# Ten instead of six pairs of layer 1's up projections by seven half-size products, summed in PSUM chains, and the scaled copies of h moved behind the last square

## The chip, the cores and the metric

The kernel runs on one core of a Trainium2 chip. Its engines are TensorE (PE for matmuls, PEld for the loads of their stationary side), VectorE (DVE), ScalarE (ACT), GpSimd (POOL) and SyncE (SP, which here only issues DMAs). The metric is device time of one execution in microseconds (us). All data are float32; most matmuls run on float32 values split into a high and a low part, three products for one.

## The reference

A trunk of two decoder layers on 512 tokens of width 1024. Layer 0 is a conformer convolution and a SwiGLU feed-forward part; layer 1 is sliding-window attention and another feed-forward part. The change lies in the second feed-forward part alone:

```python
def rmsnorm(x, g):
    return x * rsqrt(mean(x * x, -1) + EPS) * g

def swiglu_ffn(x, w_up, w_down):              # w_up: 1024 x 5632, w_down: 2816 x 1024
    gate, up = split(x @ w_up, 2, axis=-1)
    return (silu(gate) * up) @ w_down

h = h + attn @ w_o                            # the end of attention
h = h + swiglu_ffn(rmsnorm(h, norm_ffn[1]), ffn_w_up[1], ffn_w_down[1])
out = rmsnorm(h, norm_final)
```

## The kernel before

The hidden width 2816 is cut into eleven pairs of two 128-wide blocks. `STEPS1` (line 37) writes the order of layer 1 out by hand: up 0, up 1, up 2, low 0, up 3, up 4, low 2, and so on to up 9, up 10, low 8. "up p" makes the gated hidden values of pair p, "low p" multiplies two pairs, p and p + 1, with their part of `w_down` and adds to h. The last pair, 10, goes through a plain down projection at the end (line 1451).

A plain pair (`plain_pair`, line 741) takes four weight chunks of 128 x 1024 values. Each chunk is 8 weight blocks, each block three matmuls (`mm3`, line 352: high times high, high times low, low times high) over 512 tokens. A pair by sevens (`seven_pair`, line 772) multiplies in Strassen-Winograd's way: a 2 x 2 split of weights and of tokens, seven products of 256 tokens each instead of eight. It takes seven chunks: three blocks of the weights (A11, A12, A22) and four sums of blocks (S1 to S4). Against them stand B11, B21 of h and four differences of h (T1 to T4). Before the change, pairs 1, 3, 5, 6, 8 and 9 go this way (`SEVENS`, line 57), each product has a PSUM bank of its own, and ACT, DVE and POOL put the four output quarters c11, c12, c21, c22 together (lines 786 to 800). The low units (`low_pairs`, line 833) already use chains: `CHAINS` (line 827) names three banks, x, y and z. In x the products A11, S2, S3 and A22 are added one after the other, in z S1 and S4, and what stands in the bank after each is read out before the next is added.

The weights come through `advance` (line 278), called once per chunk. It moves the making of sums one step on (`prepare`, line 252: each sum takes two steps; a copy of one block inside DRAM on SP's queue, placed behind the latest load, then a transfer from POOL's queue that adds the other block in DRAM), issues loads up to six chunks ahead into four raw buffers (line 247, SP), and splits up to three chunks ahead: ACT casts raw to the high part (line 273), DVE subtracts to get the low part (line 276). Sums begin in layer 0's second feed-forward part, four for each unit by sevens, up or low.

The seam is the end of attention and pair 0. While `w_o`'s last products come out, DVE adds them to h (line 1410), and for each of h's eight row blocks `Rows.on_h` (line 719) splits the row scaled by the norm's gain (ACT line 510, DVE line 511), squares it on ACT (line 463) and adds the squares on DVE (line 467). `Rows.sums` (line 723), a generator that `plain_pair` drives in pair 0, makes eight scaled copies of h on ACT (line 726), the four differences T on POOL (line 732), and their splits on ACT and DVE (lines 515 to 519). The norm's factor goes through PE (line 477), POOL (line 481), DVE (line 484) and PE (line 503). During pair 1, eight `flip`s (line 1421) transpose h on PE.

Behind the products of a pair, DVE (line 806), ACT (807) and POOL (808) gate the hidden values, POOL makes the forms that low units need (`forms_of`, line 813, POOL line 822), and ACT and DVE split them (lines 515 to 519).

The order of instructions on each engine is made by a scheduler of the framework from the program's order and its own estimate of times. `issue_after(x)` adds an order, no wait: what is traced inside comes behind x on x's engine.

Of the kernel before, what the change touches and what calls it, by code (L numbers as in the profile page):

```python
# [14 lines left out]
ALU = mybir.AluOpType  # L15
# [8 lines left out]
FT = FF // P  # L24
# [28 lines left out]

SEVEN = ("A11 B11", "S3 T3", "S1 T1", "S2 T2", "A12 B21", "S4 B22", "A22 T4")
SEVENS = (1, 3, 5, 6, 8, 9)
SEVEN_FIRST = ("A11 B11", "S1 T1", "S3 T3", "S2 T2", "A12 B21", "S4 B22", "A22 T4")
SEVEN_LOW = ("A11 B11", "S1 T1", "S2 T2", "A12 B21", "S3 T3", "S4 B22", "A22 T4")


def by_seven(layer, pair):
    return layer == 1 and pair in SEVENS


def order_of(kind, pair):
    if kind == "low":
        return SEVEN_LOW
    return SEVEN_FIRST if pair == SEVENS[0] else SEVEN


def ups(layer, pair):
# [4 lines left out]


def blocks_of(kind, pair):
    return [(kind, pair, n.split()[0]) for n in order_of(kind, pair)]  # L80


def is_block(c):
# [116 lines left out]
def hybrid_trunk(ctx: ExitStack, tc: tile.TileContext, xT, W, prm_in, wdw_in, sinks, relb, onehot, fin, lead, out):  # L200
    nc = tc.nc
# [10 lines left out]
    def uid(s):  # L212
        ctr[0] += 1
        return f"{s}{ctr[0]}"

    def bank():
        return ps.tile([P, 512], F32, tag="bank", name=uid("bank"))

    def quad(dt=F32R):
        return quads.tile([P, 4, 512], dt, tag="quad", name=uid("quad"))  # L220

    def temp():
        return tmp.tile([P, 512], F32, tag="tmp", name=uid("tmp"))
# [69 lines left out]
    def get_seven(kind, pair, n):  # L293

        advance()
        u = stream["use"]
        stream["use"] += 1
        assert PLAN[u] == blocks_of(kind, pair)[n]
        return splits.pop(u)
# [49 lines left out]
        sh = dict(a=n)  # L349
        return tuple(w and w.rearrange("p (a b) -> p a b", **sh) for w in (hi, lo))  # L350

    def mm3(out, w, x, start, stop):
        if w[1] is None:
            nc.tensor.matmul(out, w[0], x, start=start, stop=stop)  # L354
            return
        nc.tensor.matmul(out, w[0], x[0], start=start, stop=False)  # L356
        nc.tensor.matmul(out, w[0], x[1], start=False, stop=False)  # L357
        nc.tensor.matmul(out, w[1], x[0], start=False, stop=stop)  # L358

    class Act:  # L360
        def __init__(self, n, w=512):
# [33 lines left out]
    h = [hT[:, i, :] for i in range(KT)]  # L395
# [53 lines left out]
    def col(name, i):  # L449
        c = PARAM_COLS[name] + i  # L450
        return prm[:, c:c + 1]


    class Rms:
# [5 lines left out]

        def add(self, t):
            sq = temp()[:, 0:self.w]
            nc.scalar.square(sq, t)  # L463
            if self.acc is None:
                self.acc = sq
            else:
                self.eng.tensor_add(sq, self.acc, sq)  # L467
                self.acc = sq
# [44 lines left out]
    def split(dst, src, negative=False):  # L513
        if negative:
            nc.scalar.mul(dst[0], src, -1.0)
            nc.vector.scalar_tensor_tensor(dst[1], src, -1.0, f32(dst[0]), op0=ALU.mult, op1=ALU.subtract)
            return
        nc.scalar.copy(dst[0], src)
        nc.vector.tensor_sub(dst[1], src, f32(dst[0]))
# [190 lines left out]
    class Rows:  # L710
# [12 lines left out]
        def sums(self):  # L723
            f = [quad(F32) for _ in range(2)]
            for i in range(KT):
                nc.scalar.mul(f[i // 4][:, i % 4, :], h[i], col(self.gain, i))
            b11, b12, b21, b22 = (x[:, :, s] for x in f for s in HALF)
            t1 = self.pool.tile([P, 1024], F32, tag="sum", name=uid("t1"), bufs=1).rearrange("p (k s) -> p k s", k=4)

            for name, t, f, a, b in (("T1", t1, nc.gpsimd.tensor_sub, b11, b12), ("T3", b12, nc.gpsimd.tensor_sub, b22, b12),  # L730
                                     ("T2", b11, nc.gpsimd.tensor_add, b12, b11), ("T4", b21, nc.gpsimd.tensor_sub, b11, b21)):
                f(t, a, b)
                yield
                both = quads.tile([P, 2, 4, 256], F32R, tag="quad", name=uid("rows"))
                self.block[name] = [both[:, a] for a in range(2)]
                split(self.block[name], t, name == "T2")

    def new_gates(pool):
        return pool.tile([P, 2, 2, 2, 256], F32, tag="up", name=uid("up"), bufs=3)
# [32 lines left out]
    def seven_pair(pair, rows, pool, between=None):  # L772

        c = new_gates(pool)
        c11, c12, c21, c22 = (c[:, m, s] for m in range(2) for s in range(2))
        acc = {}
        for n, name in enumerate(order_of("up", pair)):
            w = [x.rearrange("p (a k c) -> p a k c", a=2, k=4) for x in get_seven("up", pair, n)]
            a, b = name.split()
            x = rows.block[b]  # L780
            r = acc[a] = bank().rearrange("p (a s) -> p a s", a=2)
            for which in range(2):
                for k in range(4):
                    mm3(r[:, which], [v[:, which, k, :] for v in w], [x[e][:, k, :] for e in range(2)],
                        which == 0 and k == 0, which == 1 and k == 3)
            if a == "A11":
                nc.scalar.copy(c11, r)
            elif a == "S1":
                nc.scalar.copy(c22, r)
            elif a == "S2":  # L790
                nc.vector.tensor_add(c12, r, c11)
                nc.vector.scalar_tensor_tensor(c21, acc["S3"], -1.0, c12, op0=ALU.mult, op1=ALU.subtract)
                nc.gpsimd.tensor_add(c12, c12, c22)
                nc.gpsimd.tensor_sub(c22, c21, c22)
            elif a == "A12":
                nc.vector.tensor_add(c11, r, c11)
            elif a == "S4":
                nc.vector.tensor_add(c12, r, c12)
            elif a == "A22":
                nc.vector.tensor_sub(c21, c21, r)  # L800
            if between is not None:
                between()
        rs_bc = rows.rms.step2().rearrange("p (s q) -> p s q", s=2)
        for m in range(2):
            gate = c[:, m, :, 0, :]
            nc.vector.tensor_mul(gate, gate, rs_bc)
            nc.scalar.activation(gate, gate, AF.Silu)
            nc.gpsimd.tensor_mul(gate, gate, c[:, m, :, 1, :])
        return c
# [3 lines left out]
    def forms_of(c, pool, odd):  # L813
# [9 lines left out]
        for part in (slice(0, 2), slice(3, 4), slice(4, 8)):  # L823
# [3 lines left out]
    CHAINS = {"A11": ("x", 0, 0), "S1": ("z", 1, 1), "S2": ("x", 0, 1), "A12": ("y", 0, 0), "S3": ("x", 1, 1),  # L827
              "S4": ("z", 0, 1), "A22": ("x", 1, 0)}

    def rows_of(g, t):  # L830
        return hT[:, g * 4:(g + 1) * 4, t * P:(t + 1) * P]

    def low_pairs(pair, forms, rs):

        chains = {}
        for n, name in enumerate(order_of("low", pair)):
            whi, wlo = get_seven("low", pair, n)
            a, b = name.split()
            chain, g, s = CHAINS[a]
            first = chain not in chains  # L840
            if first:
                chains[chain] = [bank() for _ in range(2)]
            for t, out in enumerate(chains[chain]):
                for e in range(2):
                    xh, xl = (f[:, FORM[b], t * P:(t + 1) * P] for f in forms[e])
                    ws = slice(e * 512, (e + 1) * 512)
                    for i, (x, w) in enumerate(((xh, whi), (xh, wlo), (xl, whi))):
                        nc.tensor.matmul(out, x, w[:, ws], start=first and e == 0 and i == 0, stop=e == 1 and i == 2,  # L848
                                         skip_group_check=True)
                to, scale = rows_of(g, 2 * s + t), (rs[1] if g else rs[0])[:, 2 * s + t:2 * s + t + 1]  # L850
                src = out.rearrange("p (i c) -> p i c", i=4)
                if a == "A12":
                    m = temp()
                    nc.scalar.mul(m, out, scale)
                    nc.gpsimd.tensor_add(to, to, m.rearrange("p (i c) -> p i c", i=4))
                else:
                    nc.vector.scalar_tensor_tensor(to, src, scale, to, op0=ALU.mult, op1=ALU.add)
# [22 lines left out]
    with tc.tile_pool(name="conv", bufs=2) as cv:  # L880
# [234 lines left out]
        first = [Pw1(0, 0, raw, turn=True)]  # L1115
# [104 lines left out]
    if True:  # L1220
        ffn_part(0, 1, x0["ffn0"], ALL, Both(), nxt.on_h)
        x, rms = nxt.x, nxt.rms
# [31 lines left out]
        for n in range(4):  # L1254
            nc.vector.tensor_scalar(vq[:, n].rearrange("p a g c -> p (a g c)"), vb[n][:, 0:256], rs[:, n:n + 1], None,
                                    op0=ALU.mult)
# [126 lines left out]
        for part in range(2):  # L1383
            for g in range(2):
# [23 lines left out]
                for m in range(4):  # L1408
                    i = g * 4 + m
# [19 lines left out]
    for kind, pair in STEPS1:  # L1429
# [6 lines left out]
        if by_seven(1, pair):  # L1436
            c = seven_pair(pair, nxt, pool7, flip if pair == SEVENS[0] else None)
        else:
            c = plain_pair(pair, nxt, pool7)
        if pair == SEVENS[0]:  # L1440
            flip()
# [10 lines left out]
    for b in range(NBLK):  # L1452
# [3 lines left out]
        for g, (whi, wlo) in enumerate(whole):  # L1456
            acc = bank()
# [50 lines left out]
```

## Time and profile before

| | |
|---|---|
| median of 3 runs | 1071.57 us (1064.79 to 1073.39) |
| the profiled execution | 1072.48 us |
| its span, first to last instruction | 1070.1 us |
| granted TensorE clock, mean | 0.994 |
| PE busy | 1054.9 us (99%) |
| DVE, ACT, POOL busy | 748.5, 554.1, 432.8 us |
| HBM read and written | 181.64 and 51.38 MB |

The page of the profile gives busy time by engine, 40 slices of the span with the granted clock (PEclk) and the DMA engines' busy share, the DMA queues, and the chain of work that ended last. Rows of the timeline read: start in us, duration in us, engine, line, operation, output<-inputs, shape, count, and in brackets the engine's idle time before it with what ended it. A matmul's duration is its latency; matmuls overlap, so the distance of two starts is what one costs. In this execution attention ends at about 711 us, pair 0 runs to 742, layer 1's other pairs and low units to 1056.

### The profile page before, as it was taken

Reading aid. Unit: us, or ns where it says so; the run is one execution under the profiler, and the core shown is the slowest. Engines: PE = TensorE matmul, PEld = TensorE weight load, DVE = VectorE, ACT = ScalarE, POOL = GpSimd, SP = SyncE. Lnnn points to the kernel's source line nnn. Section 1 sums busy time; section 2 is a strip of 40 time slices with the busy share of each in tenths; the row PEclk is TensorE's granted clock in tenths of the full one; section 3 lists DMA queues with packets and bytes.
Section 4 is the critical chain, followed back from the end, with each engine's and each line's share of the span. In section 5 each row is a group of like instructions: output and inputs, shape, how many; then the busy total and the mean of one; then the engine's idle time right before and its main releaser. Section 6 shows DMA issues by size and latency. Waiting matters only on the chain.

```text
span 1070.1 us, 16002 instructions
## 1 busy us (share of the span) xinstructions
PE 1054.9 (99%) x5878; PEld 917.0 (86%) x5878; DVE 748.5 (70%) x1159; ACT 554.1 (52%) x968; POOL 432.8 (40%) x523
## 2 busy tenths in 40 slices
PE   9999999999999999999999999998999999999996
PEld 7888889999988888888888877777989899898985
DVE  3999988977777644444436466487767778768867
ACT  3887888755565333222343565474544355444543
POOL 3999998710321312211212344123532415315401
PEclk9999999999999999999999999998999999999998
DMA  9238046565556777676766444455989655545532
GB/s 356 86 98 98 3 141 214 178 230 184 177 183 191 236 203 211 169 211 190 189 188 188 138 109 137 118 158 158 277 229 332 213 188 179 157 156 177 180 118 79
DMA packets 52059, 187.92 MB, mean 176 GB/s; under 512 B 6188, under 2 KB 12493, under 8 KB 51277
## 3 DMA queue, kind: packets, MB, share of 16 engines
q1 hardware_dynamic: 44924, 162.74, 46.4%
q0 software_dynamic: 6336, 23.07, 12.6%
q8 instruction: 46, 0.75, 0.3%
q10 hardware_dynamic: 720, 1.10, 0.3%
q14 instruction: 33, 0.26, 0.1%
HBM read 181.64 MB, written 51.38 MB: 218 GB/s over the span
## 4 chain that ended last, share of the span: by engine, by line
PE 96%; DVE 2%; ACT 1%; issue 1%; DMA 1%; POOL 0%; SPq 0%
PE bank L356 19%; PE bank L357 19%; PE bank L358 19%; PE bank L906 10%; PE bank L848 9%; PE bank L388 5%; PE bank L354 4%; PE bank L389 3%; PE bank L1304 1%; PE bank L1346 1%; PE bank L1333 1%; PE bank L1004 1%; DMA both<-in_lead_dram 1%; PE bank L894 1%; PE bank L1461 0%
## 5 line engine op out<-in xcount | busy, mean ns | idle before, releaser
L276 DVE TENSOR_TENSOR wlo<-raw,whi 128x1024 fp32r<-128x1024 f32 x219 | 299.7, 1371 | 175.2 <-ACT whi L273 174.1
L273 ACT CAST whi<-raw 128x1024 fp32r<-128x1024 f32 x219 | 229.6, 1049 | 311.7 <-PE bank L357 199.7
L357 PE MATMUL bank<-quad,whi 128*128 128x512 f32 (+1 forms) x1008 | 349.8, 347 | 3.9 <-DVE quad L511 3.9
L356 PE MATMUL bank<-quad,whi 128*128 128x512 f32 (+1 forms) x1008 | 350.1, 348 | 0.0
L358 PE MATMUL bank<-quad,wlo 128*128 128x512 f32 (+1 forms) x1008 | 349.4, 347 | 0.0
L357 PEld LDWEIGHTS bank<-quad,whi 128*128 128x128 f32 x1008 | 191.5, 190 | 27.5 <-DVE quad L511 4.3
L356 PEld LDWEIGHTS bank<-quad,whi 128*128 128x128 f32 x1008 | 191.6, 190 | 24.8 <-issue 1.6
L358 PEld LDWEIGHTS bank<-quad,wlo 128*128 128x128 f32 x1008 | 191.5, 190 | 23.9 <-issue 0.6
L948 POOL TENSOR_TENSOR pr<-pr,pr 128x256 f32<-128x256 f32 x208 | 156.9, 812 | 6.6 <-ACT pr L947 6.6
L955 DVE SCALAR_TENSOR_TENSOR bank<-apad,wdw,bank 128x256 f32<-128x256 f32 x248 | 112.4, 484 | 3.4
L947 ACT ACTIVATE pr<-apad,wdw 128x256 f32<-128x256 f32 x208 | 98.2, 501 | 14.8 <-POOL pr L948 13.0
L906 PE MATMUL bank<-quad,w 128*128 128x256 f32 x448 | 98.7, 380 | 0.0
L906 PEld LDWEIGHTS bank<-quad,w 128*128 128x128 f32 x448 | 84.9, 190 | 11.8 <-DVE bank L955 0.2
L388 PE MATMUL bank<-quad,whi 128*128 128x512 f32 x212 | 75.9, 398 | 0.0
L268 POOL DMA_DIRECT2D sum<-in_W_dram x22 | 18.3, 833 | 123.0 <-DMA sum<-in_W_dram 122.8
L822 POOL TENSOR_TENSOR up<-up 128x256 f32<-128x256 f32 x40 | 44.2, 1114 | 43.0 <-DVE up L768 41.4
L268 POOL DMA_DIRECT2D sum<-sum x22 | 18.0, 818 | 105.8 <-DMA sum<-in_W_dram 104.3
L389 PE MATMUL bank<-quad,wlo 128*128 128x256 f32 x212 | 59.3, 280 | 0.0
L467 POOL TENSOR_TENSOR tmp<-tmp,tmp 128x256 f32<-128x256 f32 (+1 forms) x28 | 27.0, 963 | 79.1 <-ACT tmp L463 62.8
L848 PE MATMUL bank<-wlo,fhi 128*128 128x512 f32 x140 | 55.1, 393 | 0.0
L356 PE MATMUL bank<-rows,whi 128*128 128x256 f32 x192 | 54.6, 285 | 0.0
L358 PE MATMUL bank<-rows,wlo 128*128 128x256 f32 x192 | 54.3, 283 | 0.0
(220 smaller groups left out, 1603.3 us busy)
## 6 DMA issues: line engine op xcount, KB each, us to landing
raw<-in_W_dram SPq DMA_DIRECT2D x187, 512.0 KB, 3.8
sum<-in_W_dram SPq DMA_DIRECT2D x44, 512.0 KB, 5.4
raw<-sum SPq DMA_DIRECT2D x44, 512.0 KB, 3.9
sum<-in_W_dram POOLq DMA_DIRECT2D x22, 512.0 KB, 6.6
sum<-sum POOLq DMA_DIRECT2D x22, 512.0 KB, 6.4
w<-in_W_dram SPq DMA_DIRECT2D x14, 512.0 KB, 9.0
fd<-fs SPq DMA_DIRECT2D x1, 3072.0 KB, 34.1
h<-in_xT_dram SPq DMA_DIRECT2D x8, 256.0 KB, 8.4
```

The lines of the kernel that those rows point to most:

```text
L273: on_act = nc.scalar.copy(hi, src).ins
L276: latest[:] = [on_act, lo_engine[0].tensor_sub(lo, src, f32(hi)).ins]
L356: nc.tensor.matmul(out, w[0], x[0], start=start, stop=False)
L357: nc.tensor.matmul(out, w[0], x[1], start=False, stop=False)
L358: nc.tensor.matmul(out, w[1], x[0], start=False, stop=stop)
L388: nc.tensor.matmul(first[2], first[0], first[1], start=start, stop=False)
L389: nc.tensor.matmul(second[2], second[0], second[1], start=False, stop=stop)
L848: nc.tensor.matmul(out, x, w[:, ws], start=first and e == 0 and i == 0, stop=e == 1 and i == 2, skip_group_check=True)
L906: mm = nc.tensor.matmul(self.pb[:, w * W2:(w + 1) * W2], w1_of(ct, w, k), x[k] if x else xg[k][:, tok], start=k == 0, stop=k == KT - 1)
L947: on_act = nc.scalar.mul(pr, a[:, j:j + W2], tap(j))
L948: on_pool = nc.gpsimd.tensor_add(pr, acc, pr)
L955: on_dve = nc.vector.scalar_tensor_tensor(yt if i == nd - 1 else c, src, tap(i), c if i else self.shift, op0=ALU.mult, op1=ALU.add)
```

## The change

Three things are changed.

- All pairs of layer 1 but the first go by sevens: 2, 4, 7 and 10 join the six. Four more units are 16 more sums of weights. One order of the products holds for all, that of the low units: A11, S1, S2, A12, S3, S4, A22. `Rows.sums` makes T2 second, from B22 and T1.
- The seven products of an up pair go to three banks by `CHAINS`. What is read out: A11 is copied to c11 (ACT), S1 to c22 with the sign turned (ACT), S2 to c12 (ACT), A12 added to c11 (DVE), S3 subtracted from c22 (DVE), S4 added to c12 (DVE), A22 copied to c21 with the sign turned (ACT). The two operations on POOL and two on DVE are gone.
- ACT's eight scaled copies of h (`Rows.sums`) are ordered behind the last square of `Rows.on_h`.

```diff
--- before.py
+++ after.py
@@ -53,22 +53,13 @@
 
 
 
-SEVEN = ("A11 B11", "S3 T3", "S1 T1", "S2 T2", "A12 B21", "S4 B22", "A22 T4")
-SEVENS = (1, 3, 5, 6, 8, 9)
-SEVEN_FIRST = ("A11 B11", "S1 T1", "S3 T3", "S2 T2", "A12 B21", "S4 B22", "A22 T4")
-SEVEN_LOW = ("A11 B11", "S1 T1", "S2 T2", "A12 B21", "S3 T3", "S4 B22", "A22 T4")
-
+SEVEN = ("A11 B11", "S1 T1", "S2 T2", "A12 B21", "S3 T3", "S4 B22", "A22 T4")
+SEVENS = tuple(range(1, FT // 2))
 
 def by_seven(layer, pair):
     return layer == 1 and pair in SEVENS
 
 
-def order_of(kind, pair):
-    if kind == "low":
-        return SEVEN_LOW
-    return SEVEN_FIRST if pair == SEVENS[0] else SEVEN
-
-
 def ups(layer, pair):
     return [("up", layer, pair, half, which) for half in range(2) for which in range(2)]
 
@@ -77,7 +68,7 @@
 
 
 def blocks_of(kind, pair):
-    return [(kind, pair, n.split()[0]) for n in order_of(kind, pair)]
+    return [(kind, pair, n.split()[0]) for n in SEVEN]
 
 
 def is_block(c):
@@ -349,13 +340,13 @@
         sh = dict(a=n)
         return tuple(w and w.rearrange("p (a b) -> p a b", **sh) for w in (hi, lo))
 
-    def mm3(out, w, x, start, stop):
+    def mm3(out, w, x, start, stop, **kw):
         if w[1] is None:
             nc.tensor.matmul(out, w[0], x, start=start, stop=stop)
             return
-        nc.tensor.matmul(out, w[0], x[0], start=start, stop=False)
-        nc.tensor.matmul(out, w[0], x[1], start=False, stop=False)
-        nc.tensor.matmul(out, w[1], x[0], start=False, stop=stop)
+        nc.tensor.matmul(out, w[0], x[0], start=start, stop=False, **kw)
+        nc.tensor.matmul(out, w[0], x[1], start=False, stop=False, **kw)
+        nc.tensor.matmul(out, w[1], x[0], start=False, stop=stop, **kw)
 
     class Act:
         def __init__(self, n, w=512):
@@ -460,7 +451,7 @@
 
         def add(self, t):
             sq = temp()[:, 0:self.w]
-            nc.scalar.square(sq, t)
+            self.squared = nc.scalar.square(sq, t).ins
             if self.acc is None:
                 self.acc = sq
             else:
@@ -723,12 +714,13 @@
         def sums(self):
             f = [quad(F32) for _ in range(2)]
             for i in range(KT):
-                nc.scalar.mul(f[i // 4][:, i % 4, :], h[i], col(self.gain, i))
+                with tc.issue_after(self.rms.squared):
+                    nc.scalar.mul(f[i // 4][:, i % 4, :], h[i], col(self.gain, i))
             b11, b12, b21, b22 = (x[:, :, s] for x in f for s in HALF)
             t1 = self.pool.tile([P, 1024], F32, tag="sum", name=uid("t1"), bufs=1).rearrange("p (k s) -> p k s", k=4)
 
-            for name, t, f, a, b in (("T1", t1, nc.gpsimd.tensor_sub, b11, b12), ("T3", b12, nc.gpsimd.tensor_sub, b22, b12),
-                                     ("T2", b11, nc.gpsimd.tensor_add, b12, b11), ("T4", b21, nc.gpsimd.tensor_sub, b11, b21)):
+            for name, t, f, a, b in (("T1", t1, nc.gpsimd.tensor_sub, b11, b12), ("T2", b11, nc.gpsimd.tensor_add, b22, t1),
+                                     ("T3", b12, nc.gpsimd.tensor_sub, b22, b12), ("T4", b21, nc.gpsimd.tensor_sub, b11, b21)):
                 f(t, a, b)
                 yield
                 both = quads.tile([P, 2, 4, 256], F32R, tag="quad", name=uid("rows"))
@@ -773,31 +765,33 @@
 
         c = new_gates(pool)
         c11, c12, c21, c22 = (c[:, m, s] for m in range(2) for s in range(2))
-        acc = {}
-        for n, name in enumerate(order_of("up", pair)):
+        chains = {}
+        for n, name in enumerate(SEVEN):
             w = [x.rearrange("p (a k c) -> p a k c", a=2, k=4) for x in get_seven("up", pair, n)]
             a, b = name.split()
-            x = rows.block[b]
-            r = acc[a] = bank().rearrange("p (a s) -> p a s", a=2)
+            x, chain = rows.block[b], CHAINS[a][0]
+            first = chain not in chains
+            if first:
+                chains[chain] = bank().rearrange("p (a s) -> p a s", a=2)
+            r = chains[chain]
             for which in range(2):
                 for k in range(4):
                     mm3(r[:, which], [v[:, which, k, :] for v in w], [x[e][:, k, :] for e in range(2)],
-                        which == 0 and k == 0, which == 1 and k == 3)
+                        first and which == 0 and k == 0, which == 1 and k == 3, skip_group_check=True)
             if a == "A11":
                 nc.scalar.copy(c11, r)
             elif a == "S1":
-                nc.scalar.copy(c22, r)
+                nc.scalar.mul(c22, r, -1.0)
             elif a == "S2":
-                nc.vector.tensor_add(c12, r, c11)
-                nc.vector.scalar_tensor_tensor(c21, acc["S3"], -1.0, c12, op0=ALU.mult, op1=ALU.subtract)
-                nc.gpsimd.tensor_add(c12, c12, c22)
-                nc.gpsimd.tensor_sub(c22, c21, c22)
+                nc.scalar.copy(c12, r)
             elif a == "A12":
                 nc.vector.tensor_add(c11, r, c11)
+            elif a == "S3":
+                nc.vector.tensor_sub(c22, c22, r)
             elif a == "S4":
                 nc.vector.tensor_add(c12, r, c12)
             elif a == "A22":
-                nc.vector.tensor_sub(c21, c21, r)
+                nc.scalar.mul(c21, r, -1.0)
             if between is not None:
                 between()
         rs_bc = rows.rms.step2().rearrange("p (s q) -> p s q", s=2)
@@ -833,7 +827,7 @@
     def low_pairs(pair, forms, rs):
 
         chains = {}
-        for n, name in enumerate(order_of("low", pair)):
+        for n, name in enumerate(SEVEN):
             whi, wlo = get_seven("low", pair, n)
             a, b = name.split()
             chain, g, s = CHAINS[a]
```

## The prediction

> **What bounds the kernel now.** I read the page first (busy shares, granted clock, DMA share, chain of work), then busy time by stretch for layer 1's feed-forward part, then the timelines of PE, ACT, DVE and POOL where the page shows a dip, then the DMA queues.
>
> ```profile
> span 1070.1 us, 16002 instructions
> PE 1054.9 (99%) x5878; PEld 917.0 (86%) x5878; DVE 748.5 (70%) x1159; ACT 554.1 (52%) x968; POOL 432.8 (40%) x523
> PEclk9999999999999999999999999998999999999998
> DMA  9238046565556777676766444455989655545532
> PE 96%; DVE 2%; ACT 1%; issue 1%; DMA 1%; POOL 0%; SPq 0%
> sum<-in_W_dram SPq DMA_DIRECT2D x44, 512.0 KB, 5.4
> ```
>
> PE is the bound: 99% busy and 96% of the chain. So time falls only if PE gets fewer matmul steps or loses an idle stretch, and it rises if PE has to wait for something new. Two places in the page matter: the one slice in mid-kernel where the clock falls to 8, and three DMA slices (9, 8, 9) right behind it. The last row is the copies that begin the weight sums: 44, four for each of eleven units taken by seven products.
>
> ```profile
> 10.00:30.00 20.00, 20.00 (x97) 17.65 (x96) 10.01 (x24) 8.52 (x21) 8.00 (x12) 1.00 1.04 400
> 711.00:742.00 31.00, 27.12 (x108) 21.71 (x107) 23.22 (x19) 15.81 (x21) 13.71 (x7) 0.89 0.52 141
> 798.00:838.00 40.00, 40.00 (x257) 36.48 (x256) 30.89 (x32) 18.57 (x23) 17.91 (x16) 1.00 1.03 318
> 871.00:908.00 37.00, 37.00 (x310) 36.96 (x309) 32.05 (x33) 19.84 (x25) 16.11 (x11) 1.00 0.58 185
> ```
>
> The columns are the stretch, its length, busy time of PE, PEld, DVE, ACT and POOL, the clock, the DMA share and GB/s. In 711:742 (pair 0, the seam) PE misses 3.9 us and its clock is down. In 871:908 (pairs 5 and 6, seven products each, no sums being made) nothing is missing. In 798:838 PE is full too, but the DMA engines are at 1.03 with 318 GB/s; with plain loads alone (10:30) they moved 400.
>
> **The change, part by part.** The sum is made against the profiled execution: 1070.1 us of span and 2.4 around it, 1072.5 us, which is 0.9 above the median of the three runs (1071.57).
>
> *Products of pairs 2, 4, 7 and 10.* A plain pair is 4 chunks x 8 x 3 = 96 matmuls of 512 columns; a pair by sevens is 7 x 8 x 3 = 168 of 256 columns.
>
> ```profile
> 742.14 0.28 PE L357 MATMUL bank<-quad,whi 128*128 128x256 f32 x1
> ...
> 744.77 0.28 PE L358 MATMUL bank<-quad,wlo 128*128 128x256 f32 x1
> ```
>
> ```profile
> 767.93 0.39 PE L357 MATMUL bank<-quad,whi 128*128 128x512 f32 x1
> ...
> 771.33 0.39 PE L357 MATMUL bank<-quad,whi 128*128 128x512 f32 x1
> ```
>
> The first pair of rows lies 22 steps apart, 2.63 us, so 0.1195 us a step; the second 15 steps, 3.40 us, 0.2267. A plain pair takes 96 x 0.2267 = 21.8 us, one by sevens 168 x 0.1195 = 20.1. Four pairs save 4 x 1.7 = 6.7 us. It is a small gain because seven products of half the width are 7/8 of the work and a step of 256 is a little over half a step of 512.
>
> *The seam.* What stops PE in 711:742 is one DVE instruction:
>
> ```profile
> 720.59 0.61 PE L356 MATMUL bank<-quad,whi 128*128 128x512 f32 x2
> 725.08 0.50 PE L357 MATMUL bank<-quad,whi 128*128 128x512 f32 x1 [3.88 <-DVE quad L511]
> ```
>
> ```profile
> 727.82 0.77 PE L356 MATMUL bank<-quad,whi 128*128 128x512 f32 x1
> ...
> 732.66 0.45 PE L358 MATMUL bank<-quad,wlo 128*128 128x512 f32 x1
> ```
>
> ```profile
> 711.87 0.68 DVE L1410 TENSOR_TENSOR h<-bank,h 128x512 f32<-128x512 f32 x1
> 715.62 3.19 DVE L276 TENSOR_TENSOR wlo<-raw,whi 128x1024 fp32r<-128x1024 f32 x1 [2.47 <-ACT whi L273]
> 719.40 2.88 DVE L467 TENSOR_TENSOR tmp<-tmp,tmp 128x512 f32<-128x512 f32 x1
> 722.21 2.82 DVE L511 SCALAR_TENSOR_TENSOR quad<-h,prm,quad 128x512 fp32r<-128x512 f32 x1
> ```
>
> ```profile
> 715.04 2.68 POOL L732 TENSOR_TENSOR t<-quad 128x1024 f32<-128x1024 f32 x1
> 719.24 2.49 POOL L732 TENSOR_TENSOR quad<-quad,quad 128x1024 f32<-128x1024 f32 x1 [1.52 <-ACT quad L726]
> ```
>
> ```profile
> 710.87 3.78 ACT L726 ACTIVATE quad<-h,prm 128x512 f32<-128x512 f32 x6
> 714.55 1.03 ACT L273 CAST whi<-raw 128x1024 fp32r<-128x1024 f32 x1
> 715.49 0.72 ACT L510 ACTIVATE quad<-h,prm 128x512 fp32r<-128x512 f32 x1
> ```
>
> The last row of h is ready at 712.55, but ACT first makes six scaled copies (3.78 us), so the split of h's last two rows starts at 715.49. The copies also let POOL start its differences at 715.04, and DVE's instructions beside them take 2.8 to 3.2 us. So the last low half ends at 725.03 and PE idles 3.88 us. Then it runs at half speed: 4.84 us for eleven steps that take 2.49 at 0.2267, 2.35 us lost. With the copies behind the last square, ACT after 710.87 does one cast, two splits and two squares (some 3.7 us, to 714.6), DVE follows by about 716.5, and PE wants those rows at 719.2 and 720.6: no wait. I take off 3.88 + 2.35 = 6.2 us. Bounds: nothing saved (POOL's differences hit another instruction PE needs) and 7.0 (the eight tiny matmuls behind the gap also run cold). I take nearly all, since the margin is 4 us.
>
> What now comes later: eight copies at 0.63 us put T1 at about 717.5 instead of 715.0, and four POOL operations of some 2.6 us end near 729. T1's rows are wanted at the second product of pair 1, which starts at 735.4 + 2.9 with the 6.2 us gone, T2's 2.9 later (it moves up by one product), T3's at the fifth. On ACT the casts of pair 0 wait behind the copies, at 5.4 us a chunk; on POOL the power of the norm waits behind at most two differences, 5 us, against 8 us that it was early (it is needed with the pair's last product). Both cost nothing; if that cover goes, some 2 us.
>
> For the clock, the gap of 3.88 us is the only one in mid-kernel and the half-speed steps follow it. The Trainium skill, TensorE: Matmul & The Clock Gate, Part 1, says that an idle window of about 3.4 us drops the clock to half. By that rule shorter waits cost their own length only and the sum stays as it is; if waits elsewhere gather to that length, each would cost about 2.35 us more.
>
> *Evacuations and chains.* The six old pairs lose three DVE/POOL steps and gain two ACT copies (0.58 us each); POOL loses two operations per pair. The four new ones add three casts (1.05) and three subtractions each, while PE's time per pair stays 20 us and DVE is at 32 of 37 in 871:908 where all pairs are of this kind. Nothing here is a bound: 0 us. One wait is new: product 3 writes the bank of product 1, 5 that of 3, 7 that of 5, so each evacuation must be done within one product, 2.9 us.
>
> ```profile
> 868.07 1.05 ACT L273 CAST whi<-raw 128x1024 fp32r<-128x1024 f32 x1 [1.70 <-PE bank L357]
> 869.02 0.58 ACT L787 COPY up<-bank 128x512 f32<-128x512 f32 x1
> ```
>
> A cast stands in front of the copy on ACT: 1.05 + 0.58 of 2.9 us, so 1.2 us to spare. It holds, as long as the cast's own data are there.
>
> *The sums of weights.* Four more units are 16 more copies on SP's queue, 16 more accumulating transfers on POOL's, and 12 more loads on SP's. One sum starts every second chunk, so their pace is set by PE.
>
> ```profile
> q1 hardware_dynamic: 1959, 9.55, 60.2%
> q0 software_dynamic: 864, 3.15, 42.6%
> ```
>
> ```profile
> sum<-in_W_dram SPq DMA_DIRECT2D x35, 512.0 KB, 5.2
> ```
>
> ```profile
> 825.60 1.05 ACT L273 CAST whi<-raw 128x1024 fp32r<-128x1024 f32 x1 [3.38 <-DMA raw<-in_W_dram]
> ```
>
> ```profile
> 787.59 16.48 PE bank L848 x72
> ```
>
> The first two rows are the queues in 798:838, the third the copies issued up to 766, where pair 2 begins. At 0.524 MB a transfer, q1 moved 18.2 and q0 6.0 in 40 us: exactly the mix of a sum and its two loads (three to one), so the full DMA engines need 6.6 us per sum. PE asks for one per two chunks: 5.74 us in a pair, and 5.5 in a low unit (12 matmuls of 0.229 a chunk, by the last row). Before, pair 2 and pair 4 were plain, 21.8 us for two sums, and the engines caught up. Now chunks follow at 2.8 us from pair 2 on with 60 - 35 = 25 sums to make: 50 chunks, 5 pairs x 20.1 + 2 low units x 19.2 + 2.9 = 141.8 us of PE against 25 x 6.6 = 165: 23 us too much. How much is buffered? Before, the lag grew from 787.6 at 1.0 in 5.6, and at 825.6 a cast waited for its load for the first time: 6.8 us. Behind that PE had up to two more chunks in split form, 5.7 us, or only the 1.2 us of the evacuations when a cast that waits stands in front of the copy. So PE waits 10.7 to 15.2 us; below, nothing (more traffic can't help). I take 11, since in the only row of a late cast PE did not idle.
>
> Sum: 1072.5 - 6.7 - 6.2 + 11 = 1070.6 us.
>
> **The rivals.**
>
> *The transfers stay hidden, 1059.6 us.* If loads overtake sums or the engines keep 400 GB/s as in 10:30, the 11 fall away: 1072.5 - 12.9. For it: four transfers of 0.524 MB in 5.7 us are 368 GB/s, less than 400. Against: 1.03 of share at 318, and the cast that waited. The Trainium skill, DMA: Bandwidth & Descriptors, Specifications, gives 435 GB/s as the ceiling of the fabric; by that rule 368 would fit and this rival would hold, but the row of 318 at a full share, with accumulating transfers in it, speaks against it.
>
> *Slower: POOL waits for copies, ACT for POOL, PE for ACT, 1085 us.*
>
> ```profile
> POOL sum L268 <- DMA sum<-in_W_dram: 37.4, 8, 8.7
> ACT fhi L515 <- POOL up L822: 11.6, 4, 3.6
> ```
>
> From 765 to 1050 POOL stood up to 8.7 us in front of an accumulating transfer whose copy had not landed, with the forms (L822) queued behind it, and ACT up to 3.6 us for those. Before, an ACT copy behind that cost PE nothing, each product having its own bank. In the chains anything over 1.2 us stops PE: 2.4 to 7.5 us at a pair's start, so some 3 us for each of pairs 3 to 6 beyond the DMA's 11 makes +12 to +15, about 1085. Against: PSUM evacuations in low units have the same chains and run without a gap.
>
> *The seam stays shut, 1076.8 us.* The order on the engines is made by a scheduler; if DVE's splits still meet POOL's differences, the 6.2 us stay.
>
> **How the numbers follow.** Forecast 0.52, hidden transfers 0.18, slower 0.2, seam unchanged 0.1. A measurement tells about 1% here, 10.7 us: faster means under 1060.9, which only the first rival and the lowest edge of the forecast reach; slower means over 1082.3. That gives 0.2 faster, 0.59 same, 0.21 slower. The range 1059 to 1084 takes in the hidden case and the forecast with 15.2 and an unchanged seam (1081), and leaves out the upper part of the slow rival. The forecast's own range is 1064 to 1076.
>
> **What would show it.** Right: no idle PE and full clock behind pair 0; T1 starting later than ACT's last square; 168 matmuls at 0.12 us in pairs 2, 4, 7, 10; DMA share near 1.0 from pair 2 to pair 6; casts waiting for loads and PE idle before a first matmul on a chunk or on a chained bank, all before the last sum lands. Wrong: a DMA share under 0.95 there, PE full throughout, or PE waits on ACT where the loads are early.

## The result, and the profile after

The changed kernel takes 1074.04 us (median of 20 runs, 1071.9 to 1076.39) against 1070.95 before: a ratio of 1.0035, 95% interval 1.0023 to 1.0048. It is a little slower; the forecast was a little faster, 1070.6. The profiled execution took 1071.9, the lowest of its runs, while that of before stands 1.5 us above its median.

The page of the changed kernel, in the lines that were shown of before:

```profile
span 1070.1 us, 16696 instructions
PE 1050.4 (98%) x6166; PEld 924.1 (86%) x6166; DVE 747.6 (70%) x1163; ACT 579.1 (54%) x1008; POOL 435.1 (41%) x535
PEclk9999999999999999999999999999999999999998
DMA  9248045675566777676766444457999999965552
```

The 8 in the clock's row is gone from the seam, and the DMA engines now stand at 9 for seven slices. The stretches show what was given and what was taken. Columns as before: stretch, length, busy time of PE, PEld, DVE, ACT, POOL, clock, DMA share, GB/s. First the kernel before, from where the changed kernel begins pair 2 to where its last sum lands:

```profile
757.00:930.00 173.00, 173.00 (x1034) 154.65 (x1034) 130.48 (x136) 78.90 (x95) 70.75 (x57) 1.00 0.76 231
```

then the changed kernel, at the seam and there:

```profile
711.00:742.00 31.00, 31.00 (x175) 26.87 (x174) 24.28 (x23) 20.30 (x28) 16.30 (x9) 1.00 0.60 168
757.00:930.00 173.00, 165.10 (x1107) 150.85 (x1106) 128.58 (x132) 88.36 (x113) 75.29 (x69) 0.99 1.03 323
```

The seam is full of work at full clock. In 757:930 the DMA share went from 0.76 to 1.03, and PE is idle for 7.9 of 173 us.

The seam in the changed kernel, ACT, DVE, POOL and PE in turn:

```profile
713.23 5.02 ACT L718 ACTIVATE quad<-h,prm 128x512 f32<-128x512 f32 x8
```

```profile
714.43 0.74 DVE L502 SCALAR_TENSOR_TENSOR quad<-h,prm,quad 128x512 fp32r<-128x512 f32 x1
...
721.83 3.42 DVE L510 TENSOR_TENSOR rows<-t,rows 128x1024 fp32r<-128x1024 f32 x1
```

```profile
715.93 2.41 POOL L724 TENSOR_TENSOR t<-quad 128x1024 f32<-128x1024 f32 x1 [1.90 <-ACT quad L718]
```

```profile
733.20 0.68 PE L347 MATMUL bank<-quad,whi 128*128 128x256 f32 x1
```

The eight copies come behind the last square, the last low half of h is done at 715.17 (725.03 before), POOL starts when DVE has got past it, and the slowed DVE instruction is now one that PE does not wait for. Pair 1 begins at 733.20; before, its first matmul stood at 741.62.

```profile
741.62 0.68 PE L356 MATMUL bank<-quad,whi 128*128 128x256 f32 x1
```

That is 8.4 us earlier, about one of them gained ahead of the seam. From there to the end of the span the kernel before takes 328.5 us, the changed one 336.9, and the changed one without any sums (below) 322.5. So four pairs by sevens are worth 6.0 us in the traces, and 14.4 us were lost behind the seam, nearly all while sums were made. The DMA queues of the changed kernel in 757:930, and all that PE waited for there:

```profile
q1 hardware_dynamic: 8559, 41.66, 60.8%
q0 software_dynamic: 3867, 14.10, 41.8%
```

```profile
PE bank L842 <- DVE wlo L267: 5.7, 4, 3.6
PE bank L347 <- ACT up L786: 0.9, 2, 0.7
PE bank L347 <- ACT whi L264: 0.6, 2, 0.4
PE bank L349 <- DVE wlo L267: 0.6, 1, 0.6
```

The numbers behind a colon are the sum of the waits, how many there were and the longest, in us. At 0.524 MB each, q0 moved 26.9 accumulating transfers in 173 us, 6.4 us per sum. PE waited 6.9 us for weights and 0.9 for a readout. How a late load reaches PE, ACT and then PE:

```profile
809.26 1.05 ACT L264 CAST whi<-raw 128x1024 fp32r<-128x1024 f32 x1 [3.49 <-DMA raw<-in_W_dram]
810.22 0.58 ACT L786 COPY up<-bank 128x512 f32<-128x512 f32 x1
```

```profile
809.88 0.28 PE L347 MATMUL bank<-quad,whi 128*128 128x256 f32 x1
810.85 0.39 PE L347 MATMUL bank<-rows,whi 128*128 128x256 f32 x1 [0.69 <-ACT up L786]
```

ACT stands 3.5 us in front of a cast whose load is late, the readout of S2's product (line 786) waits behind it though its data are there, and PE cannot add the next product to that bank. The largest wait has one link more: POOL, DVE, PE.

```profile
850.78 1.45 POOL L802 TENSOR_TENSOR up<-up 128x512 f32<-128x512 f32 x1
...
855.88 0.83 POOL L816 TENSOR_TENSOR up<-up 128x256 f32<-128x256 f32 x1
```

```profile
851.27 7.67 DVE L267 TENSOR_TENSOR wlo<-raw,whi 128x1024 fp32r<-128x1024 f32 x2
```

```profile
857.86 0.50 PE L842 MATMUL bank<-wlo,fhi 128*128 128x512 f32 x1 [3.56 <-DVE wlo L267]
...
859.03 0.63 PE L842 MATMUL bank<-whi,flo 128*128 128x512 f32 x1
859.45 0.63 PE L842 MATMUL bank<-wlo,fhi 128*128 128x512 f32 x1
```

Six operations ran on POOL without a pause, and the first of two subtractions on DVE took 6.5 us in place of 1.2 beside them. PE idled 3.56 us, and from 858.7 to 862.1 its steps of 512 columns are some 0.43 us apart in place of 0.23, half the clock.

### The profile page after: what moved, and what is told of

Same layout as the page of the kernel before. It is cut to its first block, busy times and chain, and to the rows that moved or that the text cites. A ratio compares the mean times of both kernels' runs of the same rounds, so it can differ in the third digit from the quotient of the medians.

```text
span 1070.1 us, 16696 instructions
## 1 busy us (share of the span) xinstructions
PE 1050.4 (98%) x6166; PEld 924.1 (86%) x6166; DVE 747.6 (70%) x1163; ACT 579.1 (54%) x1008; POOL 435.1 (41%) x535
## 5 line engine op out<-in xcount | busy, mean ns | idle before, releaser
L267 DVE TENSOR_TENSOR wlo<-raw,whi 128x1024 fp32r<-128x1024 f32 x231 | 314.5, 1366 | 189.7 <-ACT whi L264 189.2
L264 ACT CAST whi<-raw 128x1024 fp32r<-128x1024 f32 x231 | 241.6, 1049 | 286.1 <-PE bank L348 171.6
L349 PE MATMUL bank<-quad,wlo 128*128 128x256 f32 (+1 forms) x976 | 326.5, 335 | 0.7 <-DVE wlo L267 0.6
L347 PE MATMUL bank<-quad,whi 128*128 128x256 f32 (+1 forms) x976 | 326.7, 336 | 0.4 <-ACT whi L264 0.4
L348 PE MATMUL bank<-quad,whi 128*128 128x256 f32 (+1 forms) x976 | 326.0, 334 | 0.0
L347 PEld LDWEIGHTS bank<-quad,whi 128*128 128x128 f32 x976 | 185.3, 190 | 20.4 <-issue 1.6
L348 PEld LDWEIGHTS bank<-quad,whi 128*128 128x128 f32 x976 | 185.3, 190 | 18.1 <-issue 0.2
L941 ACT ACTIVATE pr<-apad,wdw 128x256 f32<-128x256 f32 x208 | 98.3, 501 | 14.8 <-POOL pr L942 12.9
L347 PE MATMUL bank<-rows,whi 128*128 128x256 f32 x320 | 91.2, 285 | 2.0 <-ACT up L786 1.2
L349 PE MATMUL bank<-rows,wlo 128*128 128x256 f32 x320 | 90.5, 283 | 0.0
L348 PE MATMUL bank<-rows,whi 128*128 128x256 f32 x320 | 90.5, 283 | 0.0
L259 POOL DMA_DIRECT2D sum<-sum x30 | 24.6, 820 | 132.3 <-DMA sum<-in_W_dram 131.0
L802 POOL TENSOR_TENSOR up<-up 128x512 f32<-128x512 f32 x20 | 33.0, 1649 | 106.2 <-ACT up L801 106.2
L347 PEld LDWEIGHTS bank<-rows,whi 128*128 128x128 f32 x320 | 61.3, 192 | 3.2 <-ACT up L786 1.8
```

Of the source, the lines that this page charges most:

```text
L259: nc.gpsimd.dma_start(summed[a], chunk(a, SUMS[a[2]][1]), accum_op=ALU.add, max_dma_last_dim=4096)
L264: on_act = nc.scalar.copy(hi, src).ins
L267: latest[:] = [on_act, lo_engine[0].tensor_sub(lo, src, f32(hi)).ins]
L347: nc.tensor.matmul(out, w[0], x[0], start=start, stop=False, **kw)
L348: nc.tensor.matmul(out, w[0], x[1], start=False, stop=False, **kw)
L349: nc.tensor.matmul(out, w[1], x[0], start=False, stop=stop, **kw)
```

## Experiments

Three theories. D: the sums ask more of the DMA engines than they have, and all the loss hangs on that. C: the chains' readouts are a wait of their own. S: what the seam gives is given back where the sums are made. Each median stands against before's median beside it (1069.9 to 1071.3); where two kernels were not timed side by side, that spread leaves about 1 us open. "Pair 1 to the end" is the time in a trace from pair 1's first matmul to the end of the span, one execution each.

**The seam alone**, on the kernel before:

```diff
-            nc.scalar.square(sq, t)
+            self.squared = nc.scalar.square(sq, t).ins
...
-                nc.scalar.mul(f[i // 4][:, i % 4, :], h[i], col(self.gain, i))
+                with tc.issue_after(self.rms.squared):
+                    nc.scalar.mul(f[i // 4][:, i % 4, :], h[i], col(self.gain, i))
```

> The kernel before with one edit: ACT's eight scaled copies of h behind the last square. If the seam's idle time and half clock are simply removed, 6 to 8 us less than before (ratio 0.993 to 0.994), PE full from pair 0 on and pair 1 starting at about 734. Rival: what the seam gives is given back where sums are made, because PE arrives there earlier and the DMA engines are full at the two plain pairs too: then within 2 us of before.

1065.2 us against 1070.66: 0.9956 (0.9939 to 0.9973). Pair 1 begins at 734.27, PE has no wait behind it, pair 1 to the end takes 328.5 us as before, and nothing is given back. The 5.5 us are a little under the 6 to 8 expected; between the two traces they are 7.3. What the seam costs differs from run to run: beside this kernel the runs of before lie between 1064.48 and 1073.88, its own between 1063.95 and 1065.84, and the five shortest of before have a mean clock of 0.997 or 0.998, as all of its own do. So some runs of before seem to lose next to nothing at the seam; none of those was traced.

**The changed kernel without the seam's order** (the same lines undone):

> The changed kernel without the order on ACT. If the DMA engines bound the stretch of the sums and its start moves with PE, 6 to 8 us slower than the changed kernel, so about 1.0 to 1.1% slower than before. Rival: the loss and the seam overlap (a PE that comes later finds more sums done), then within 2 us of the changed kernel, 0.3% slower than before.

1079.3: 1.0092 (1.0057 to 1.0127), so 5.3 us over the changed kernel's median, a little under the 6 to 8 expected, with an interval of some 4 us either way. The old gap is back, and the loss behind it is there too (336.4 us from pair 1 to the end, 336.9 in the changed kernel):

```profile
725.57 0.80 PE L348 MATMUL bank<-quad,whi 128*128 128x512 f32 x1 [3.87 <-DVE quad L502]
```

S falls by both runs: the seam is worth some 5 us with or without the extra sums.

**Chains and seam with the six pairs of before:**

```diff
-SEVENS = tuple(range(1, FT // 2))
+SEVENS = (1, 3, 5, 6, 8, 9)
```

> The changed kernel with the six pairs of before: chains and seam, no more sums. If chains cost nothing while loads are early, the same as the seam alone (6 to 8 us less than before). If the readouts of the chains are the loss (three hand-overs a pair at some 0.5 us or more), 9 us or more lost in six pairs: equal to before or slower.

1065.12: 0.9959 (0.994 to 0.9978), the same as the seam alone. With loads early, no price of the chains shows in the time (one wait of 0.2 us in the trace): C as a price of its own falls.

**Ten pairs, seam, a bank for each product** (the kernel of the first experiment with the changed kernel's `SEVENS`; the products keep their old order too):

> The kernel before with the seam's edit and ten pairs by sevens, each product in its own bank as before: more sums without chains. If the DMA engines are the loss, within 3 us of the changed kernel (0 to 0.5% slower than before). If the chains are, at least 8 us faster than the changed kernel, 0.5% or more faster than before.

1070.47: 1.0006 (0.9988 to 1.0024). That is 3.6 us less than the changed kernel, between the two expectations. Its stretch in 757:930, and all that PE waited for there:

```profile
757.00:930.00 173.00, 165.37 (x1120) 151.12 (x1119) 143.42 (x145) 82.77 (x102) 93.91 (x79) 1.00 1.03 326
```

```profile
PE bank L358 <- DVE wlo L276: 3.6, 4, 1.8
PE bank L849 <- DVE wlo L276: 2.0, 4, 1.1
PE bank L849 <- DVE h L858: 1.6, 2, 1.3
PE bank L356 <- ACT whi L273: 0.4, 1, 0.4
```

The DMA share is the same 1.03, as D would have it. 6.0 us of the waits are for weights and 1.6 for readouts in low units, none is longer than 1.8 us, and the clock stays at 1.00. Over the whole span the ten runs have a mean clock of 0.996 to 0.998, the twenty of the changed kernel 0.994 to 0.996. Late loads cost 11.6 us over the kernel without sums (next) where products have banks, and 15.2 where they share chains.

**No sums at all** (a plain block of the weights is loaded where a sum would be, so another result is computed):

```diff
-        return summed[c] if is_sum(c) else W[CHUNK_AT[c]]
+        return W[CHUNK_AT[c[:2] + ("A11",) if is_sum(c) else c]]
...
-    preparing[0] = prepare()
```

> The changed kernel without the making of the sums: no copies and no accumulating transfers in DRAM, and where a sum would be loaded the first block of the weights is loaded instead (its time is read, what it computes is not the reference's). If the DMA engines are the loss, PE is full behind pair 0, the DMA share about 0.6, and the time 1058 to 1060, 13 us less than before (ratio 0.988). If chains or the readouts lose the time, 1066 or more.

1058.85: 0.9889 (0.9841 to 0.9938). PE is full, and pair 1 to the end takes 322.5 us:

```profile
757.00:930.00 173.00, 173.00 (x1212) 162.28 (x1212) 130.33 (x142) 96.38 (x122) 54.82 (x42) 1.00 0.56 184
```

**The copies without the accumulating transfers** (the sums lack their second block):

```diff
-                nc.gpsimd.dma_start(summed[a], chunk(a, SUMS[a[2]][1]), accum_op=ALU.add, max_dma_last_dim=4096)
```

> The changed kernel with the copies that begin the sums, without the accumulating transfers on POOL's queue (the sums lack their second block, so what it computes is not the reference's). By the queues' rates a sum and its two loads then take 3 x 1.3 = 3.9 us of the DMA engines against 5.7 us of PE: no wait, 1058.5 to 1060. If the copies and the order on SP's queue are the cost, 1066 or more.

1058.18: 0.9884 (0.9853 to 0.9915), as without any sums.

```profile
757.00:930.00 173.00, 173.00 (x1212) 162.29 (x1211) 130.75 (x142) 96.57 (x122) 53.81 (x42) 1.00 0.74 260
```

The copies take the DMA share from 0.56 to 0.74, the accumulating transfers from there to 1.03: they are what fills the engines. D is shown twice. This second kernel also loses POOL's waits in front of those transfers (77.9 us in 757:930 of the changed kernel), so by itself it would leave open which of the two is the cost; but ACT's casts waited 37.6 us for late loads there in the changed kernel, and not once in these two.

**Sums begun 38 chunks earlier:**

```diff
+    preparing[0] = prepare()
     pw2(h1.z, n1)
...
-    preparing[0] = prepare()
```

> The changed kernel with the sums started earlier, at layer 0's second output projection of the convolution instead of its second feed-forward part: 38 chunks earlier, 19 sums more done before pair 1. If the DMA engines are the loss, the last sum lands at about 800 instead of 930, little of the 14 us is lost, and the time is 1060 to 1064. If the loss moves into layer 0 (POOL standing in front of transfers there), 1068 or more with idle PE between 250 and 350.

1061.86: 0.9915 (0.9891 to 0.994), 12 us less than the changed kernel. The last sum lands at about 814. But layer 0 now has full engines, and PE misses 1.3 us there:

```profile
250.00:340.00 90.00, 88.66 (x575) 80.09 (x574) 60.89 (x77) 47.85 (x79) 32.25 (x32) 1.00 1.02 326
```

**Each cast behind ACT's readout of the product four chunks earlier**, on the changed kernel:

```diff
-        on_act = nc.scalar.copy(hi, src).ins
+        with tc.issue_after(freed) if freed else nullcontext():
+            on_act = nc.scalar.copy(hi, src).ins
...
-            split_weights(hi, lo, raws.pop(i))
+            split_weights(hi, lo, raws.pop(i), readout.get(i - 4))
...
-                nc.scalar.copy(c11, r)
+                readout[stream["use"] - 1] = nc.scalar.copy(c11, r).ins
```

> The changed kernel with each cast of a weight chunk on ACT ordered behind the readout of the product four chunks earlier. If the chains' own part of the loss (some 3.5 us between ten pairs with banks and with chains) is a cast that waits for its load in front of a readout, 1070 to 1072, like ten pairs with banks. If that part is something else (the gap of 3.6 us and its half clock at 854, which is DVE beside POOL), no change: 1074.

1071.83: 1.0019 (0.9999 to 1.004), 2.2 us less than the changed kernel, inside the first expectation; the two intervals overlap. All that PE waits for in 757:930:

```profile
PE bank L352 <- DVE wlo L270: 1.8, 3, 0.8
PE bank L845 <- DVE wlo L270: 1.3, 3, 0.5
PE bank L350 <- ACT up L789: 1.2, 1, 1.2
PE bank L845 <- DVE h L854: 0.3, 1, 0.3
```

The waits for readouts have not become less: 1.5 us, against 0.9 in the changed kernel. What is gone is the wait of 3.56 us and the half clock behind it, and the ten runs have a mean clock of 0.995 to 0.998. So the order on ACT helps, but the trace does not bear out that it does so by earlier readouts; how it moved the long wait away is not shown.

**A slower pace in layer 0 and a faster one in the wide chunks behind it**, on the changed kernel with the sums begun 38 chunks earlier:

```diff
+            made += 1
-            yield
-            yield
+            for _ in range(4 if made < 10 else 1 + made % 2 if made < 50 else 2):
+                yield
```

> The changed kernel with sums begun 38 chunks earlier, as in the early one, but slower there (one per four chunks, ten sums) and faster in the wide chunks that follow (three chunks for two sums, forty sums), two chunks again at the end. If the rest of the early version's loss against the kernel without sums (3 us) is the full DMA engines in layer 0 and at 800 to 816, 1059 to 1060.5. If it is the sums as such, 1062 again.

1060.92: 0.9909 (0.9878 to 0.994), inside neither expectation (1059 to 1060.5, or 1062). PE is full in both stretches, with the engines at 0.86 in layer 0 and at 0.70 in the sevens:

```profile
250.00:340.00 90.00, 90.00 (x587) 81.95 (x587) 60.89 (x78) 49.25 (x81) 29.21 (x26) 1.00 0.86 270
...
757.00:930.00 173.00, 173.00 (x1213) 162.29 (x1212) 131.25 (x143) 97.30 (x124) 59.77 (x49) 1.00 0.70 226
```

**The same pace with a bank for each product:**

> The same pace of sums in the kernel with ten pairs and a bank for each product. If chains cost nothing with loads early, within 1 us of the paced version with chains; if readouts on DVE and POOL cost, 2 us slower; if chains still cost, 2 us faster.

1059.0: 0.9895 (0.9862 to 0.9928), 2 us less than the paced chains. The next pair tells whether that is casts in front of readouts:

> The paced version with chains and the casts behind the readouts. If the 2 us by which the paced chains stood behind the paced banks (1060.9 against 1059.0) are casts in front of readouts, 1059. If they are chance or belong to something else, 1061, and PE's waits stay where they were (750).

> The paced version with a bank for each product once more, beside the one above on the same chip and in more rounds, so that chains and banks can be told apart: 1059, and 0 to 2 us less than the one above.

Paced chains with the casts behind the readouts: 1060.64, 0.9909 (0.9885 to 0.9933). Paced banks once more: 1060.16, 0.991 (0.9886 to 0.9934). By their times they can't be told apart. The traces still differ a little: with chains PE waits 0.8 us in the first (for one of ACT's readouts in pair 1) and 1.9 us in the second (1.0 of them for such a readout), in both traces with banks never. Both beat the kernel before by 0.9% and the changed kernel by 1.2%: with the sums spread, the seam and the four pairs bring some 10 of the 12.9 us forecast for them.

## Why the prediction was wrong

The direction was wrong by a small margin: the terms of the sum come to 1.9 us less than before (-6.7 - 6.2 + 11), measured are 3.1 more. The step that failed is one, the 11 us of "so PE waits 10.7 to 15.2 us ... I take 11, since in the only row of a late cast PE did not idle." The changed kernel stands 15.2 us over the kernel without sums (1074.04 and 1058.85). The other terms were 1 us too favourable together, and the profile that the sum starts from, 1072.5, was an execution 1.5 us above the median of the twenty (1070.95).

- *The products*, 6.7 us: the kernel without sums is 6.35 us under the seam alone with its six pairs (1058.85 and 1065.2, timed on different chips), and 6.0 us by the traces behind the seam. Right.
- *The seam*, 6.2 us: right in mechanism (the splits done 10 us earlier, no gap, full clock), and 5.5 measured. Nothing that now comes later cost PE time there.
- *Evacuations and chains*, 0 us with loads early: right in the time; six pairs in chains equal six in banks. (Four steps on DVE and POOL went from each old pair, not three.)
- *The sums' demand*: right. 25 x 6.6 = 165 us were worked out from pair 2 on; the measured pace is 6.4 us for 26.9 accumulating transfers, since pair 2 now begins earlier, and the last sum lands some 173 us after it.
- *The buffer behind it* is what was mis-sized. The two ends had been worked out for a reason: 5.7 us if PE can use up its split chunks, 1.2 us if a waiting cast stands in front of a readout. The row from which I chose came from a kernel in which a readout could be late at no cost, since each product had its own bank. It could not decide about chains. Ten pairs with banks lost 11.6 us, which is the end that I took; ten with chains lost 15.2; with the casts behind the readouts 13.0.
- That the loss fell on the other end, 15.2, is in part luck. That end rested on readouts that stop PE, and PE waited for readouts only 0.9 of 7.9 us in 757:930. What the chains lost beyond the banks goes with the clock: the medians of the runs' clocks are 0.995 in the changed kernel and 0.997 with banks, and 0.2% of 1070 us is some 2 us of the 3.6 (an estimate). The sum had put half clock behind the seam at nothing.
- *The slow rival* had two of its links (a queue in front of a readout, POOL bunched by late copies) but not their size. The 3.56 us wait came through DVE beside POOL. On the clock the trace agrees with the rule that was cited (the Trainium skill, TensorE: Matmul & The Clock Gate, Part 1): 3.56 us was followed by half the clock, the waits of 1.4 us and less (1.8 with ten banks) were not.
- *The first rival* would have needed 368 GB/s. The engines gave 323 at a share of 1.03, so the ceiling of 435 (the Trainium skill, DMA: Bandwidth & Descriptors, Specifications) was not what bounded these transfers. The prediction took that row alone; the next row of the same table, ~358 GB/s for the HBM of one core, would not have let 368 through, though the loads of 10:30 went at 400.

What stays open is why the six operations on POOL meet a subtraction that PE needs in the chains and not in the banks, and the rest of the 3.6 us, some 1.5 us: readouts on ACT or on DVE, or the order of the products, and no run tells them apart.

## What to carry to other kernels

When the matmuls of a stage shrink, work out what the same transfers then ask of the DMA engines per microsecond, kind by kind, and where the lead is used up; a plain stage that looks slow may be where they catch up. A readout that shares an in-order engine with casts that wait for loads is late whenever those are, so before a bank is shared, ask what stands in front of its readout. Work that can be done ahead goes where the engines have room: here beginning the sums earlier, at a pace set by stage, was worth 13 us and no matmul changed. And a wait is priced with the clock behind it, by the granted clock of every run and not of the traced one alone.

## What the runs showed of the hardware

- An accumulating transfer of 512 KB cost far more of the DMA engines than a plain one: in 798:838 of before 42.6% of 40 us for 6.0 of them, 2.8 us each, against 1.3 us for loads and copies. With one in four of that kind the engines were full at 318 to 326 GB/s; loads alone moved 400 (10:30 of before).
- A subtraction on DVE over 128 x 1024 values with two inputs in SBUF took 1.2 us alone, 2.7 to 3.4 beside operations of POOL at the seam, and 6.5 beside six in a row, in the changed kernel and in the one without the seam's order alike. Each of the long ones ended 1.1 us behind the end of an operation on POOL (857.80 and 856.71, 721.91 and 720.83), as if it had run only then; why it came in between two of them at the seam and not among the six is open.
- Stopping PE for 3.56 us was followed by half the clock for 3.4 us, for 3.88 us (before) by half the clock for 6.8, and for 3.87 us (without the seam's order) for some 10: stops of nearly one length, three lengths of half clock.
